# The layout of the second layer's normalised tokens: by position in the chunk, restored at the copies out of PSUM

## The chip, the cores and the metric

One core of one Trainium2 chip runs the whole program. The metric is the device time of one execution in microseconds. The core has TensorE (matrix products, PE in the profile; PEld is its weight loads), VectorE (DVE), ScalarE (ACT), GpSimd (POOL) and the queue SyncE (SP), which only issues DMAs here.

## What is computed

A two-layer streaming encoder step for one prompt of 2048 tokens and eight streams of 16 tokens, 2176 tokens of width 1024 in all, in float32. Layer 0 is a diagonal state-space mixer, layer 1 a gated delta rule. Cut to what the change touches, layer 1 is:

```
h    = rms_norm(x, norm_g[1]) * (1 + scale) + shift            # scale, shift from c
proj = h @ w_in                                                # 1024 -> 3088
qkv, z, b_raw, a_raw = split(proj)                             # 2048, 1024, 8, 8
full = concat([conv_hist, qkv], axis=1)
conv = sum(full[:, j:j + L] * conv_w[j] for j in range(4))     # along the tokens
act  = silu(conv)                                              # q, k, v of the heads
o, S = gated_delta_rule(q, k, v, sigmoid(b_raw), g(a_raw), S0)
out  = (rms_norm(o, norm_g) * silu(z)) @ w_out
```

The product `h @ w_in` runs over tokens in any order; the convolution needs them in order.

## The kernel before, in words

*Layout of the tokens.* 2176 tokens are 272 chunks of 8 (256 of the prompt, 16 of the streams). Layer 0 works by position in the chunk: its output for position j of all 272 chunks is one tile of 272 columns, and it runs through the positions backwards, j from 0 to 7 for position 7 - j. What layer 1 needs is normalised there and stored to DRAM as `h_d`, rows by channel, `[1024, position, 272]`. Position 0, the last, stays in SBUF.

*The tiles of layer 1.* For each of the 8 channel blocks k of 128 there is a high part `h1h` and a low part `h1l` (`h = h1h + h1l`, both of the type that the products take), in three tiles each by group g of chunks (`CG`, L840): 128, 96 and 48 chunks. `slots` (L836) gives the view of such a tile by position `s` and chunk `c`. `load_h(k)` (L854) loads one k from `h_d` into `xk`; `split_h` (L848) then writes, for each group, the high part by a cast on ScalarE (L851) and the low part by a subtraction on an engine E (L852), VectorE unless `load_h` is given another. k = 0 to 2 are loaded while layer 0 still runs, k = 3 to 7 at L1303 and L1312; k = 5 and 7 are split by GpSimd. k = 5 and 6 are loaded into tiles of layer 0's last products; k = 7 shares its tile `xk` with k = 3.

*Block 0 of the projection.* `first_block(k)` (L1294) multiplies the first 128 columns of `w_in` with positions 1 to 7 of channel block k, for five pieces of tokens (`NATT`: 512, 512, 384, 384, 384, of which 7/8 is 448 and 336), three products each: high by high, high weights by low, low weights by high. It accumulates over k in five PSUM tiles, in an order that is written out (`T.ordered`). Between k = 0 and 1 stand the products of the last position's norm. At the end position 0 is normalised on VectorE and ScalarE (L1314 to L1323, results `gh`, `gl`), multiplied (`pc_s`, L1324), and copied into the first position of the tiles `h1h` and `h1l`, by ScalarE (L1329) and GpSimd (L1330).

*Blocks 1 to 15, b/a and the gate.* `conv_block(b)` multiplies all tokens of a piece by 128 more columns (L1374), copies the result out of PSUM on ScalarE (L1378; L1380 for the tokens of the streams) into one row of tokens `pb`, and runs the convolution on VectorE (L1386, L1388), silu, squares (`sqf`) and stores on ScalarE. TensorE sums the squares (`pr`, L1407) inside the next block. In blocks 2 to 8 ScalarE also brings a copy of layer 0's output into token order (`x1_order`, L1427: load `x1k` on SP, copy `x1n` at L1433, store). The next weights come from `load_blk` (L842): a load `wdr` on SP, a cast on ScalarE (L135), a subtraction on VectorE (L137). `gate_cols` (L1587) does the same for the gate's eight blocks with silu straight out of PSUM, and the loop at L1460 for the 16 columns b/a.

*The order.* A scheduler places the instructions of each engine by its own estimate of when their inputs are ready, apart from stretches that the program orders by hand; each engine and each DMA queue then runs its list in that order.

The step of the moving operand in block 0 and the view that the splits write are these two lines:

```
1297    h, l = (t[k].rearrange("p (c s) -> p s c", s=8)[:, 1:8] for t in hcols(n0, n))
 838    return [t[g].rearrange("p (c s) -> p s c", s=8) for t in h]
```

Of the kernel before, what the change touches and what calls it, by code (L numbers as in the profile page):

```python
# [13 lines left out]
AF = mybir.ActivationFunctionType  # L14
# [39 lines left out]
def kernel(ctx: ExitStack, tc: tile.TileContext, I, O, upto="Z"):  # L54
# [19 lines left out]
    T, V, S, G, SY = (Engine(e) for e in (nc.tensor, nc.vector, nc.scalar, nc.gpsimd, nc.sync))  # L74
# [158 lines left out]
    with ExitStack() as pa:  # L233
# [337 lines left out]
        for j in range(8):  # L571
            hh, hl = hcur
            T.ordered = j == 1
            for cb in range(8):
# [14 lines left out]
                if j > 0:  # L589
                    ps = psd4.tile([P, NCH], F32, tag="d", name=f"pd{j}_{cb}")  # L590
# [221 lines left out]
    with ExitStack() as px:  # L812
# [20 lines left out]
                 for g in order for k in ks_ for i in "hl"}  # L833
            return [[[t[k, i, g] for g in range(3)] for i in "hl"] for k in ks_]

        def slots(h, g):  # L836

            return [t[g].rearrange("p (c s) -> p s c", s=8) for t in h]

        CG = (slice(0, 128), slice(128, 224), slice(224, NCH))  # L840

# [5 lines left out]

        def split_h(h, s0, sn, src, E):  # L848
            for g in range(3):
                hv, lv = (t[:, s0:s0 + sn] for t in slots(h, g))  # L850
                S.copy(hv, src[:, :, CG[g]])  # L851
                E.tensor_sub(lv, src[:, :, CG[g]], hv.bitcast(F32))  # L852

# [55 lines left out]
        for j in range(8):  # L909
# [3 lines left out]
            for ob in range(8):  # L913
                zt = (c4 if j else c3).tile([P, NCH], F32, tag="zt", name=f"zt{j}_{ob}")
                nc.sync.dma_start(zt, z_d[j][ob])
                ps = psc.tile([P, NCH], F32, tag="d", name=f"pg{j}_{ob}")
# [13 lines left out]
            else:  # L930
# [14 lines left out]
                hh_ = h_tiles((hpa, hpa, hpa), range(3), (0, 1, 2))  # L945
# [20 lines left out]
            for ob in range(8):  # L966
                if ob > 1:
                    project_out(ob)
                ps = pso_[ob]
# [304 lines left out]
    with pd:  # L1274
# [2 lines left out]
        hpb1 = rpool(ph1, "hpb1", 1)  # L1277
        hh_ += h_tiles((hpb1, hpb, hpb), range(3, KC), (0, 2, 1))

        def hcols(n0, n):  # L1280

            g = sum(8 * q.stop <= n0 for q in CG)
            c = n0 - 8 * CG[g].start
            return [[h[i][g][:, c:c + n] for h in hh_] for i in range(2)]

        psmp.__exit__(None, None, None)
        pd1 = pd.enter_context(ExitStack())
# [6 lines left out]
        def first_block(k):  # L1294
            for i in (0, 3, 4, 1, 2):
                n0, n = NATT[i]
                h, l = (t[k].rearrange("p (c s) -> p s c", s=8)[:, 1:8] for t in hcols(n0, n))
                ps = first[i][:, 0:7 * n // 8]
                T.matmul(ps, lhsT=wnext[0][:, k], rhs=h, start=(k == 0), stop=False)
                T.matmul(ps, lhsT=wnext[0][:, k], rhs=l, start=False, stop=False)  # L1300
                T.matmul(ps, lhsT=wnext[1][:, k], rhs=h, start=False, stop=(k == KC - 1))

        lds = [load_h(3), load_h(4), load_h(5, G), load_h(6)]  # L1303
        T.ordered = True
        first_block(0)
        norm(pss.tile([P, 512], F32, tag="s", name="msc")[:, 0:NCH])
# [2 lines left out]
        for k in range(3, KC):  # L1309
            lds[k - 3](hh_[k])  # L1310
            if k == 3:
                lds.append(load_h(7, G))  # L1312
            first_block(k)
        V.tensor_mul(xs, xs, bc(r[:, NPC:NCH].rearrange("p (q h) -> p q h", h=2), 1, 8))  # L1314
        V.tensor_mul(xs, xs, bc(gs1[:, :, 1:9], 3, 2))
# [9 lines left out]
        T.ordered = False  # L1325
        for g in range(3):
            for k in range(KC):
                hv, lv = (t[:, 0] for t in slots(hh_[k], g))
                S.copy(hv, h0[0][:, k, CG[g]].bitcast(F32))  # L1329
                G.tensor_copy(lv, h0[1][:, k, CG[g]].bitcast(F32))  # L1330
        xap.__exit__(None, None, None)
# [18 lines left out]
        def conv_block(b, w, hooks={}):  # L1350
            hi, lo = w
            pbt = pbp.tile([P, 2204], F32, tag="pb", name=f"pb_{b}")
            G.memset(pbt[:, 0:3], 0.0)
            pbs = pbt[:, 2051:2203].rearrange("p (q s) -> p q s", q=8)
            G.tensor_copy(pbs[:, :, 0:3], hist[:, b])
            sqf = i_ = None
            if b < 8:
                sqf = sqp.tile([P, NTOK], F32, tag="sqf", name=f"sqf{b}")
            for i0, (n0, n) in enumerate(NATT):
                npr = min(n, 2048 - n0)  # L1360
                if b == 0:

                    ps, c0 = first[i0][:, 0:7 * n // 8].rearrange("p (s c) -> p c s", s=7), n0 // 8
                    pv = pbt[:, 3 + n0:3 + n0 + npr].rearrange("p (c s) -> p c s", s=8)
                    S.copy(pv[:, :, 1:8], ps[:, 0:npr // 8])
                    S.copy(pv[:, :, 0], first0[:, c0:c0 + npr // 8])
                    if npr < n:
                        for h in range(2):
                            S.copy(pbs[:, :, 4 + 8 * h:11 + 8 * h],
                                   ps[:, npr // 8:].rearrange("p (q h) s -> p q h s", h=2)[:, :, h])  # L1370
                            S.copy(pbs[:, :, 3 + 8 * h], first0[:, NPC:NCH].rearrange("p (q h) -> p q h", h=2)[:, :, h])
                else:
                    ps = psd1.tile([P, 512], F32, tag="d", name=f"pc{b}_{n0}")[:, 0:n]
                    i_ = mm3(ps, [hi[:, k] for k in range(KC)], [lo[:, k] for k in range(KC)],  # L1374
                             *hcols(n0, n))
                    for f in hooks.get(i0, ()):
                        f(i_)
                    S.copy(pbt[:, 3 + n0:3 + n0 + npr], ps[:, 0:npr])  # L1378
                    if npr < n:
                        S.copy(pbs[:, :, 3:19], ps[:, npr:n].rearrange("p (q s) -> p q s", q=8))  # L1380
                ac = d3.tile([P, 512], F32, tag="ac", name=f"ac{b}_{n0}")[:, 0:n]
                parts = [(ac[:, 0:npr], lambda j: pbt[:, n0 + j:n0 + j + npr])]
                if npr < n:
                    parts.append((ac[:, npr:n].rearrange("p (q s) -> p q s", q=8), lambda j: pbs[:, :, j:j + 16]))
                for o, src in parts:
                    V.tensor_scalar(o, src(0), convw[:, b, 0:1], None, op0=ALU.mult)  # L1386
                    for j in range(1, 4):
                        V.scalar_tensor_tensor(o, src(j), convw[:, b, j:j + 1], o, op0=ALU.mult, op1=ALU.add)  # L1388
                S.activation(ac, ac, AF.Silu)
                if b < 8:  # L1390
                    store_heads(kq_d, (b + 4) % 8, n0, n, ac)
                    S.activation(sqf[:, n0:n0 + n], ac, AF.Square)
                else:
                    store_heads(v_d, b - 8, n0, n, ac)
            G.tensor_copy(hout[:, b, 0:3], pbt[:, 2048:2051])
            G.tensor_copy(hout[:, b, 3:27].rearrange("p (q s) -> p q s", q=8), pbs[:, :, 16:19])
            if b >= 8:
                return None
            rw = sqp.tile([P, 512], F32, tag="rw", name=f"rw{b}")


            def sums(after):
                pr = pss.tile([P, 512], F32, tag="s", name=f"pr{b}")
                pl = pss.tile([P, 4], F32, tag="s", name=f"prl{b}")
                with tc.issue_after(after):
                    for tt in range(4):
                        T.matmul(pr[32 * tt:32 * tt + 32, :], lhsT=one1, rhs=sqf[:, tt * 512:(tt + 1) * 512],  # L1407
                                 start=True, stop=True, tile_position=(0, 32 * tt))
                    T.matmul(pl, lhsT=sqf[:, 2048:2176], rhs=one1[:, 0:4], start=True, stop=True)
                V.tensor_copy(rw, pr)  # L1410
                V.tensor_copy(ssq[:, 16, b:b + 1], pl[:, 0:1])

            def turned(after):
                pt = pss.tile([P, 4, P], F32, tag="s", name=f"prt{b}")
                with tc.issue_after(after):
                    for o in range(4):
                        T.transpose(pt[:, o, :], rw[:, o * P:(o + 1) * P], ident)
                V.tensor_copy(ssq[:, 0:16, b].rearrange("p (t o) -> p o t", o=4),
                              pt.rearrange("p o (t r) -> p o t r", r=32)[:, :, :, 0])

            return sums, turned, i_

        with ExitStack() as pq:
# [37 lines left out]
            br = pbp.tile([P, 2204], F32, tag="pb", name="br")  # L1461
            for i0, (n0, n) in enumerate(NATT):
                ps = psd1.tile([P, 512], F32, tag="d", name=f"pba{n0}")[0:32, 0:n]
                hh, hl = hcols(n0, n)
                for k in range(KC):
                    T.matmul(ps, lhsT=wcat[:, k, :], rhs=hh[k], start=(k == 0), stop=False)
                    i_ = T.matmul(ps[0:16], lhsT=wcat[:, k, 0:16], rhs=hl[k], start=False, stop=(k == KC - 1)).ins
                S.copy(br[0:32, n0:n0 + n], ps)
                if i0 in (1, 3):
                    rows_of[7][i0 // 2](i_)  # L1470

# [115 lines left out]
        def gate_cols(b, w, n0, n, pool, tag):  # L1587
            ps = pool.tile([P, 512], F32, tag=tag, name=f"pz{b}_{n0}")[:, 0:n]
            mm3(ps, [w[0][:, k] for k in range(KC)], [w[1][:, k] for k in range(KC)], *hcols(n0, n))
            ac = d3.tile([P, 512], F32, tag="ac", name=f"az{b}_{n0}")[:, 0:n]  # L1590
            silu = S.activation(ac, ps, AF.Silu).ins
            store_heads(zz_d, b - 16, n0, n, ac)
            return silu

# [460 lines left out]
```

## Time and profile before

| what | value |
|---|---|
| device time, median of 3 runs | 2189.59 us (2188.38 to 2193.19) |
| the profiled execution's own time | 2189.92 us |
| span of the profiled execution, first to last instruction | 2188.2 us |
| mean granted clock of TensorE, share of full speed | 0.985 |
| busy: TensorE, its weight loads | 2122.6 us (97%), 1856.6 us (85%) |
| busy: VectorE, ScalarE, GpSimd | 1552.6, 962.2, 485.4 us |

The profile is of one execution. Times in its rows are microseconds from the start of the span. Layer 1 begins near 1015, block 1 of the projection at 1058, and the gate's last products end near 1690. A row's "x" is a count; "idle before" is the time that the engine stood idle ahead of the row, and the name behind the arrow is what ended it. [...]

### The profile page before, as it was taken

What the parts mean: (1) busy time and instruction counts of PE and PEld (TensorE: products, weight loads), DVE (VectorE), ACT (ScalarE), POOL (GpSimd) and SP (SyncE); (2) the same over time, 40 slices, a digit from 0 to 9 for tenths busy, and PEclk for the clock granted to TensorE, in tenths of its full rate; (3) what the DMA queues carried; (4) which work ended last, traced back from release to release, by engine and by line L of the source; (5) the groups of instructions that cost most, each with busy time, mean ns of one, the idle gap of its engine ahead of it and who ended that gap; (6) DMA issues with size and microseconds to landing.
All of it is one profiled execution on the core that took longest, in us unless ns stands there. A gap on an engine that the chain in (4) does not pass through costs nothing. (4 is left out here: it accounts for less than half of the span.)

```text
span 2188.2 us, 41752 instructions
## 1 busy us (share of the span) xinstructions
PE 2122.6 (97%) x15601; PEld 1856.6 (85%) x15601; DVE 1552.6 (71%) x3975; ACT 962.2 (44%) x2209; POOL 485.4 (22%) x731
## 2 busy tenths in 40 slices
PE   6999999999999999999999999999999799999998
PEld 4889987778789999998787879889987688888887
DVE  7999488777775444557654669687556888888885
ACT  3543422222254444447554432332223566666663
POOL 1156410000013222222300001100011244444430
PEclk8999999999999999999999999999999899999999
DMA  9796854444473333336455322563456644454532
GB/s 274 241 304 229 253 160 136 145 139 146 129 233 126 108 108 108 116 99 215 117 175 156 103 63 72 142 167 106 133 165 200 202 124 130 139 144 144 144 111 68
DMA packets 388295, 332.36 MB, mean 152 GB/s; under 512 B 87259, under 2 KB 349931, under 8 KB 388093
## 3 DMA queue, kind: packets, MB, share of 16 engines
q1 hardware_dynamic: 259084, 226.56, 35.2%
q10 hardware_dynamic: 126192, 95.49, 13.8%
q0 software_dynamic: 2816, 7.65, 1.0%
q8 instruction: 123, 2.02, 0.4%
q14 instruction: 80, 0.65, 0.1%
HBM read 213.01 MB, written 116.61 MB: 151 GB/s over the span
## 5 line engine op out<-in xcount | busy, mean ns | idle before, releaser
L149 PE MATMUL pc<-h1h,wdh 128*128 128x512 f32 (+1 forms) x600 | 217.1, 362 | 0.0
L151 PE MATMUL pc<-h1h,wdl 128*128 128x512 f32 (+1 forms) x600 | 216.7, 361 | 0.0
L150 PE MATMUL pc<-h1l,wdh 128*128 128x512 f32 (+1 forms) x600 | 215.9, 360 | 0.0
L1388 DVE SCALAR_TENSOR_TENSOR ac<-pb,convw,ac 128x384 f32<-128x384 f32 (+3 forms) x288 | 164.3, 593 | 3.6
L149 PE MATMUL pdz<-hhz,wzh 128*128 128x272 f32 x512 | 151.7, 298 | 0.0
L150 PE MATMUL pdz<-hlz,wzh 128*128 128x272 f32 x512 | 151.5, 297 | 0.0
L151 PE MATMUL pdz<-hhz,wzl 128*128 128x272 f32 x512 | 151.1, 296 | 0.0
L149 PE MATMUL po<-gh,woh 128*128 128x272 f32 x512 | 148.1, 290 | 1.3 <-ACT gh L926 1.3
L150 PE MATMUL pg<-yl,wgh 128*128 128x272 f32 x512 | 148.3, 290 | 0.0
L149 PE MATMUL pg<-yh,wgh 128*128 128x272 f32 x512 | 147.0, 288 | 1.3 <-ACT evz L630 1.3
L151 PE MATMUL po<-gh,wol 128*128 128x272 f32 x512 | 148.1, 289 | 0.0
L150 PE MATMUL po<-gl,woh 128*128 128x272 f32 x512 | 147.5, 288 | 0.0
L151 PE MATMUL pg<-yh,wgl 128*128 128x272 f32 x512 | 147.4, 288 | 0.0
L149 PEld LDWEIGHTS pc<-h1h,wdh 128*128 128x128 f32 x600 | 114.0, 190 | 10.2 <-PE pc L151 0.8
L150 PEld LDWEIGHTS pc<-h1l,wdh 128*128 128x128 f32 x600 | 113.8, 190 | 10.1 <-issue 0.8
L151 PEld LDWEIGHTS pc<-h1h,wdl 128*128 128x128 f32 x600 | 113.9, 190 | 9.7
L149 PE MATMUL pd<-hh,wuh 128*128 128x272 f32 x384 | 112.7, 294 | 0.1
L1386 DVE TENSOR_SCALAR ac<-pb,convw 128x512 f32<-128x512 f32 (+2 forms) x96 | 39.1, 421 | 103.4 <-ACT pb L1378 62.5
L69 PE MATMUL epo<-w2h,ohi 128*128 128x512 f32 x272 | 111.7, 410 | 0.0
L150 PE MATMUL pd<-hl,wuh 128*128 128x272 f32 x384 | 110.8, 289 | 0.3 <-DVE hl L230 0.3
L151 PE MATMUL pd<-hh,wul 128*128 128x272 f32 x384 | 110.9, 289 | 0.0
L69 PE MATMUL epo<-w2h,olo 128*128 128x512 f32 x272 | 106.9, 393 | 0.0
(610 smaller groups left out, 6378.5 us busy)
## 6 DMA issues: line engine op xcount, KB each, us to landing
wa<-in_w_ada SPq DMA_DIRECT2D x32, 512.0 KB
wdr<-in_w_in SPq DMA_DIRECT2D x24, 512.0 KB
h_d<-x ACTq DMA_DIRECT2D x8, 1088.0 KB
u_d<-ev ACTq DMA_DIRECT2D x64, 136.0 KB
hz<-h_d SPq DMA_DIRECT2D x16, 544.0 KB
u<-u_d SPq DMA_DIRECT2D x16, 544.0 KB
z_d<-evz ACTq DMA_DIRECT2D x64, 136.0 KB
y_d<-y ACTq DMA_DIRECT2D x32, 272.0 KB
```

Of the source, the lines that this page charges most:

```text
L69: i_ = f(*a, **kw)
L149: T.matmul(ps, lhsT=w_hi[k], rhs=x_hi[k], start=(k == 0), stop=False)
L150: T.matmul(ps, lhsT=w_hi[k], rhs=x_lo[k], start=False, stop=False)
L151: i_ = T.matmul(ps, lhsT=w_lo[k], rhs=x_hi[k], start=False, stop=(k == n - 1))
L1386: V.tensor_scalar(o, src(0), convw[:, b, 0:1], None, op0=ALU.mult)
L1388: V.scalar_tensor_tensor(o, src(j), convw[:, b, j:j + 1], o, op0=ALU.mult, op1=ALU.add)
```

## The change

The tiles `h1h` and `h1l` are kept as `p (s c)`: all chunks' tokens of position 0 first, then those of position 1, and so on, within each group. The splits and the copies of position 0 then write neighbouring words. `hcols` hands out a view of positions and chunks, 8 (or, in block 0, 7) runs of 64 or 48 neighbouring words, or one run where a piece is a whole group. A piece's result stands in PSUM in that order, and the copies out of PSUM, and the gate's silu, read it back by token. Besides, the splits of k = 5 and 7 go from GpSimd to VectorE.

```diff
-        def slots(h, g):
+        def slots(t, g):
-            return [t[g].rearrange("p (c s) -> p s c", s=8) for t in h]
+            return t[g].rearrange("p (s c) -> p s c", s=8)
...
         def split_h(h, s0, sn, src, E):
             for g in range(3):
-                hv, lv = (t[:, s0:s0 + sn] for t in slots(h, g))
+                hv, lv = (slots(t, g)[:, s0:s0 + sn] for t in h)
                 S.copy(hv, src[:, :, CG[g]])
                 E.tensor_sub(lv, src[:, :, CG[g]], hv.bitcast(F32))
...
-        def hcols(n0, n):
+        def hcols(n0, n, s0=0):
             g = sum(8 * q.stop <= n0 for q in CG)
-            c = n0 - 8 * CG[g].start
-            return [[h[i][g][:, c:c + n] for h in hh_] for i in range(2)]
+            c = slice(n0 // 8 - CG[g].start, (n0 + n) // 8 - CG[g].start)
+            return [[slots(h[i], g)[:, s0:, c] for h in hh_] for i in range(2)]
+        def by_token(ps, n):
+            return ps.rearrange("p (s c) -> p c s", c=n // 8)
...
-                h, l = (t[k].rearrange("p (c s) -> p s c", s=8)[:, 1:8] for t in hcols(n0, n))
+                h, l = (t[k] for t in hcols(n0, n, 1))
...
-        lds = [load_h(3), load_h(4), load_h(5, G), load_h(6)]
+        lds = [load_h(3), load_h(4), load_h(5), load_h(6)]
...
-                lds.append(load_h(7, G))
+                lds.append(load_h(7))
...
-                    S.copy(pbt[:, 3 + n0:3 + n0 + npr], ps[:, 0:npr])
+                    pv = by_token(ps, n)
+                    S.copy(pbt[:, 3 + n0:3 + n0 + npr].rearrange("p (c s) -> p c s", s=8), pv[:, 0:npr // 8])
                     if npr < n:
-                        S.copy(pbs[:, :, 3:19], ps[:, npr:n].rearrange("p (q s) -> p q s", q=8))
+                        S.copy(pbs[:, :, 3:19].rearrange("p q (h s) -> p q h s", h=2),
+                               pv[:, npr // 8:].rearrange("p (q h) s -> p q h s", h=2))
...
-                S.copy(br[0:32, n0:n0 + n], ps)
+                S.copy(br[0:32, n0:n0 + n].rearrange("p (c s) -> p c s", s=8), by_token(ps, n))
...
-            silu = S.activation(ac, ps, AF.Silu).ins
+            silu = S.activation(ac.rearrange("p (c s) -> p c s", s=8), by_token(ps, n), AF.Silu).ins
```

What this does to the order of the instructions is shown at three places. In the rows, `h1l_0` is the low part in group 0, the number behind it tells the tiles of one k apart, and `xk_12813`, `xk_12816` and `xk_12875` are the loads of k = 5, 6 and 7.

VectorE, from the reciprocal of the last position's norm to the end of the splits, in the kernel before:

```order
L990 RECIPROCAL acc_12475<-acc_12475 128x272
L137 TENSOR_TENSOR wdl_13111<-wdr_13112,wdh_13110 128x1024
L1314 TENSOR_TENSOR xa_12473<-xa_12473,acc_12475 128x8x16
L1321 SCALAR_TENSOR_TENSOR xa_12473<-acc_12475,gs_171,xa_12473 128x256
L1315 TENSOR_TENSOR xa_12473<-xa_12473,gs_171 128x8x16
L852 TENSOR_TENSOR h1l_0_12769<-xk_12816,h1h_0_12768 128x7x128
L1316 TENSOR_TENSOR xa_12473<-xa_12473,dsh 128x8x16
L852 TENSOR_TENSOR h1l_1_12789<-xk_12816,h1h_1_12788 128x7x96
L852 TENSOR_TENSOR h1l_2_12779<-xk_12816,h1h_2_12778 128x7x48
L1321 SCALAR_TENSOR_TENSOR xa_12473<-acc_12475,gs_171,xa_12473 128x256 x7
L1323 SCALAR_TENSOR_TENSOR gl_12993<-xa_12473,modT,gh_12992 128x272 x8
```

The same place with the change, from the first split behind the weights' (the line numbers are three higher from here on):

```order
L852 TENSOR_TENSOR h1l_0_12767<-xk_12813,h1h_0_12766 128x896
L1317 TENSOR_TENSOR xa_12473<-xa_12473,acc_12475 128x8x16
L1324 SCALAR_TENSOR_TENSOR xa_12473<-acc_12475,gs_171,xa_12473 128x256
L852 TENSOR_TENSOR h1l_1_12787<-xk_12813,h1h_1_12786 128x672
L852 TENSOR_TENSOR h1l_2_12777<-xk_12813,h1h_2_12776 128x336
L852 TENSOR_TENSOR h1l_0_12769<-xk_12816,h1h_0_12768 128x896
L852 TENSOR_TENSOR h1l_1_12789<-xk_12816,h1h_1_12788 128x672
L1318 TENSOR_TENSOR xa_12473<-xa_12473,gs_171 128x8x16
L852 TENSOR_TENSOR h1l_2_12779<-xk_12816,h1h_2_12778 128x336
L852 TENSOR_TENSOR h1l_0_12771<-xk_12875,h1h_0_12770 128x896
L852 TENSOR_TENSOR h1l_1_12791<-xk_12875,h1h_1_12790 128x672
L852 TENSOR_TENSOR h1l_2_12781<-xk_12875,h1h_2_12780 128x336
```

The splits of k = 5 and 7 now stand on VectorE, before seven of the eight operations at L1324 (L1321 before) and all eight at L1326 (L1323 before); a split is one run of elements instead of seven rows.

GpSimd, from the last sums of the norm on, as a difference:

```order
 L982 TENSOR_TENSOR acc_12475<-acc_12475,sqc 128x272 x6
-L852 TENSOR_TENSOR h1l_0_12767<-xk_12813,h1h_0_12766 128x7x128
-L852 TENSOR_TENSOR h1l_1_12787<-xk_12813,h1h_1_12786 128x7x96
-L852 TENSOR_TENSOR h1l_2_12777<-xk_12813,h1h_2_12776 128x7x48
-L852 TENSOR_TENSOR h1l_0_12771<-xk_12875,h1h_0_12770 128x7x128
-L852 TENSOR_TENSOR h1l_1_12791<-xk_12875,h1h_1_12790 128x7x96
-L852 TENSOR_TENSOR h1l_2_12781<-xk_12875,h1h_2_12780 128x7x48
```

Only the casts of position 0 are left there.

TensorE, at the end of the 24 products `pc_s` of position 0 and the start of block 1 (`pc_0` is block 1's first piece), in the kernel before:

```order
L69 MATMUL pc_s<-gh_12992,wdh_12417 128x272
L69 MATMUL pc_s<-gl_12993,wdh_12417 128x272
L69 MATMUL pc_s<-gh_12992,wdl_12418 128x272
L149 MATMUL pc_0_13191<-h1h_0_12399,wdh_13110 128x512
L150 MATMUL pc_0_13191<-h1l_0_12400,wdh_13110 128x512
L151 MATMUL pc_0_13191<-h1h_0_12399,wdl_13111 128x512
```

And with the change, from the thirteenth `pc_s` on:

```order
L69 MATMUL pc_s<-gh_12992,wdh_12417 128x272
L149 MATMUL pc_0_13191<-h1h_0_12399,wdh_13110 128x512
L150 MATMUL pc_0_13191<-h1l_0_12400,wdh_13110 128x512
L151 MATMUL pc_0_13191<-h1h_0_12399,wdl_13111 128x512
L149 MATMUL pc_0_13191<-h1h_0_12401,wdh_13110 128x512
L69 MATMUL pc_s<-gl_12993,wdh_12417 128x272
L69 MATMUL pc_s<-gh_12992,wdl_12418 128x272
L69 MATMUL pc_s<-gh_12992,wdh_12417 128x272
L150 MATMUL pc_0_13191<-h1l_0_12402,wdh_13110 128x512
L151 MATMUL pc_0_13191<-h1h_0_12401,wdl_13111 128x512
L149 MATMUL pc_0_13191<-h1h_0_12403,wdh_13110 128x512
```

Before, all 24 `pc_s` stand ahead of block 1; with the change, eleven of them stand behind its first products, and 14 products of block 1 stand ahead of the last `pc_s`. Past block 2 the order on TensorE is the same, and on SP's queue it is the same throughout.

## Rows read from the trace of the kernel before

**Rows 1.** The page's shares of the span: busy time, share and instructions by engine.
```profile
PE 2122.6 (97%) x15601; PEld 1856.6 (85%) x15601; DVE 1552.6 (71%) x3975; ACT 962.2 (44%) x2209; POOL 485.4 (22%) x731
```

**Rows 2.** Stretches: length, busy PE, PEld, DVE, ACT, POOL, then clock, DMA, GB/s.
```profile
1015.60:1036.00 20.40, 20.40 (x67) 13.19 (x66) 17.22 (x24) 17.47 (x22) 7.47 (x5) 1.00 0.66 231
...
1161.00:1223.40 62.40, 56.36 (x272) 47.94 (x271) 29.52 (x58) 30.66 (x41) 1.42 (x8) 0.95 0.57 169
```

**Rows 3.** Timeline of TensorE in block 0: start, duration, line, operation.
```profile
1022.08 0.57 PE L69 MATMUL pc<-h1h,wdl 128*128 128x448 f32 x1
1022.46 0.48 PE L69 MATMUL pc<-h1h,wdh 128*128 128x336 f32 x1
1022.74 0.48 PE L69 MATMUL pc<-h1l,wdh 128*128 128x336 f32 x1
```

**Rows 4.** The same timeline in block 1; one matmul left out between each two.
```profile
1058.14 0.39 PE L149 MATMUL pc<-h1h,wdh 128*128 128x512 f32 x1
...
1058.59 0.39 PE L151 MATMUL pc<-h1h,wdl 128*128 128x512 f32 x1
...
1070.08 0.33 PE L149 MATMUL pc<-h1h,wdh 128*128 128x384 f32 x1
...
1070.43 0.33 PE L151 MATMUL pc<-h1h,wdl 128*128 128x384 f32 x1
```

**Rows 5.** Groups by shape, ScalarE and VectorE, 993 to 1062: busy, mean ns.
```profile
L851 ACT CAST h1h<-xk 128x896 fp32r<-128x896 f32 x6 | 11.7, 1946 | 2.4 <-DMA xk<-h_d 2.4
...
L135 ACT CAST wdh<-wdr 128x1024 fp32r<-128x1024 f32 x3 | 3.1, 1044 | 2.5 <-PE pc_s L69 2.0 <-DMA wdr<-in_w_in 0.6
...
L852 DVE TENSOR_TENSOR h1l<-xk,h1h 128x896 fp32r<-128x896 f32 x4 | 7.8, 1959 | 2.9 <-ACT h1h L851 2.9
...
L137 DVE TENSOR_TENSOR wdl<-wdr,wdh 128x1024 fp32r<-128x1024 f32 x3 | 3.6, 1206 | 7.7 <-ACT wdh L135 7.7
```

**Rows 6.** Timeline of VectorE, 1028 to 1053, equal operations merged.
```profile
1028.96 1.85 DVE L990 RECIPROCAL acc<-acc 128x272 f32<-128x272 f32 x1
...
1031.80 2.66 DVE L1314 TENSOR_TENSOR xa<-xa,acc 128x128 f32<-128x128 f32 x1
...
1046.62 2.85 DVE L1321 SCALAR_TENSOR_TENSOR xa<-acc,gs,xa 128x256 f32<-128x256 f32 x7
1049.38 3.42 DVE L1323 SCALAR_TENSOR_TENSOR gl<-xa,modT,gh 128x272 fp32r<-128x272 f32 x8
```

**Rows 7.** Timeline of GpSimd in the same stretch.
```profile
1031.46 6.05 POOL L852 TENSOR_TENSOR h1l<-xk,h1h 128x896 fp32r<-128x896 f32 x3 [12.68 <-ACT h1h L851]
1038.77 7.29 POOL L852 TENSOR_TENSOR h1l<-xk,h1h 128x896 fp32r<-128x896 f32 x3 [1.25 <-ACT h1h L851]
1049.95 7.70 POOL L1330 CAST h1l<-gl 128x128 fp32r<-128x128 f32 x24 [3.90 <-DVE gl L1323]
```

**Rows 8.** Waits, 1058 to 1291: who for whom, us in total, times, longest.
```profile
ACT x1n L1433 <- DMA x1k<-x_d: 48.6, 16, 7.2
...
PE pr L1407 <- ACT sqf L1392: 5.8, 2, 4.2
```

**Rows 9.** Timeline of ScalarE behind the last product of position 0.
```profile
1058.21 1.05 ACT L135 CAST wdh<-wdr 128x1024 fp32r<-128x1024 f32 x1 [1.99 <-PE pc_s L69]
...
1067.11 2.35 ACT L1433 COPY x1n<-x1k 128x1088 f32<-128x1088 f32 x1 [7.19 <-DMA x1k<-x_d]
```

**Rows 10.** Timeline of SP's queue, 1031 to 1062.
```profile
1031.92 29.01 SPq L133 DMA_DIRECT2D wdr<-in_w_in  x2
```

**Rows 11.** Groups by shape, ScalarE's copies: busy, mean ns (1054 to 1056; 1058 to 1291).
```profile
L1365 ACT COPY pb<-pc 128x448 f32<-128x448 f32 x2 | 1.1, 560 | 0.0
...
L1378 ACT COPY pb<-pc 128x512 f32<-128x512 f32 x16 | 9.0, 579 | 2.2 <-ACT ac L1389 2.2
...
L1433 ACT COPY x1n<-x1k 128x1088 f32<-128x1088 f32 x16 | 36.9, 2309 | 48.6 <-DMA x1k<-x_d 48.6
```

**Rows 12.** Products over 256 columns, two runs and one: duration ns min/median/max.
```profile
L69 PE MATMUL epg<-ekl,ekh x48: 279/283/283, 1758.1 to 2073.8; 128*128 128x256 f32 x48
...
L69 PE MATMUL pks<-Sh,ekh x48: 278/279/388, 1772.6 to 2088.8; 128*128 128x256 f32 x48
```

More of the change, by code (lines that the diff above doesn't have):

```diff
@@ L1327 @@
             for k in range(KC):
-                hv, lv = (t[:, 0] for t in slots(hh_[k], g))
+                hv, lv = (slots(t, g)[:, 0] for t in hh_[k])
                 S.copy(hv, h0[0][:, k, CG[g]].bitcast(F32))
```

## Prediction

> **What bounds the kernel now.** I read the page's shares first: TensorE is busy for 97% of the span, VectorE for 71% [rows 1]. So a change pays where it shortens TensorE's own work, or where TensorE waits. The table of stretches says which holds around the change: in the first twenty microseconds of the second layer TensorE is busy for all 20.40 us at a granted clock of 1.00, and it is idle for 6.04 of 62.40 us between 1161 and 1223 [rows 2]. The first is the stage that the change rewrites, the second will take some of the gain back.
>
> In the first stage TensorE computes block 0 of the projection, chunk k by chunk k. From start to start, a matmul over 448 tokens takes 0.38 us and one over 336 takes 0.28 us [rows 3], so 0.84 ns a token. The same products in block 1 take 0.225 us for 512 tokens and 0.175 us for 384 (each two starts apart, halved) [rows 4], so 0.45 ns. The clock is the same and so are the types; what differs is the moving operand. In block 0 it is read as `p s c` out of a tile kept as `p (c s)`, that is, with a step of eight words between neighbours; in block 1 its tokens lie next to each other. The same step stands in the splits that write these tiles: ScalarE takes 1.946 us for 896 elements and 1.044 us for 1024 weights without a step, VectorE 1.959 against 1.206 us [rows 5]. GpSimd's splits cost VectorE more than themselves: while GpSimd works on three of them for 6.05 us [rows 7], VectorE needs 2.66 us for a product of 128 elements, against 2.85 us for seven operations of 256 elements when GpSimd is idle [rows 6].
>
> **The change, part by part.**
>
> *Block 0 on TensorE.* Each of 8 chunks k issues 3 products over 2 pieces of 448 and 3 of 336. Before: 24 x (2 x 0.38 + 3 x 0.28) = 38.4 us. After the change the operand is 7 runs of 64 or 48 neighbouring words. The price without a step comes from block 1: between 384 and 512 a token adds 0.39 ns, so 0.200 us for 448 and 0.156 us for 336. That gives 24 x (2 x 0.200 + 3 x 0.156) = 20.8 us, and TensorE has 17.6 us less to do in a stretch in which it never waits.
>
> *Whether the splits keep up.* A k takes 2.6 us then. TensorE, which begins at 1015.6, would want k = 3 near 1024 (three k and the norm's short products), then a new one every 2.6 us, up to k = 7 at 1034.5 and the products `pc_s` at 1037. ScalarE's five sets of 1904 elements cost 1.044/1024 x 1904 = 1.9 us each, about 10 us; it is not the limit. VectorE gets all five sets, 1.206/1024 x 1904 = 2.2 us each or 11.2 us, and beside them the reciprocal and the weights' split (1.85 and 1.2), eight operations at L1321 (8 x 2.85/7 = 3.3) and eight at L1323 (3.4) [rows 6], and three small ones at L1314 to L1316, which I put at 0.2 each since nothing of GpSimd's is left beside them. That is 21.5 us. It starts near 1018.5, after the last outputs of layer 0, and ends near 1040. TensorE's order needs its last result only near 1042 (the order shows that eleven of the 24 `pc_s` now stand behind products of block 1). k = 5, 6 and 7 come out of VectorE some 1.5 to 2 us ahead of their use. So I count no wait, but the margin is thin. The queue of loads on SP keeps its order; the load for k = 7 waits until k = 3 is split, and that is earlier than now. The 24 casts of the first token of a chunk stay on GpSimd; they end at 1057.65, 4.85 us behind VectorE's last operation [rows 6, 7], and TensorE needs them in their order, eight for block 1's first product, so their cover is `pc_s` and that product.
>
> *What starts later than TensorE does.* Here the gain shrinks. ScalarE's cast of the next weights waits for the last `pc_s` (1.99 us at 1058.21), and x1n, the first piece of the chain behind it, waits 7.19 us for its load [rows 9], whose place on SP's queue is behind the second weight load, held for most of 29.01 us [rows 10]. From there blocks 0 to 6 run through ScalarE, VectorE and SP at their own pace: ScalarE waits 48.6 us for x1k loads, in order, with the copies out of PSUM queued behind, and TensorE, faster, catches up and waits 5.8 us for `sqf` in the end [rows 8]. That chain begins with the last `pc_s`. TensorE is 17.6 us earlier there, but 14 products of 0.225 us now stand between the `pc_s`, so the last one ends 3.2 us later than it could: 1058.1 - 17.6 + 3.2 = 1043.7, which is 14.4 us earlier than now. TensorE then waits 3.2 us longer at `sqf`. The gain that reaches block 7 and all that follows is 14.4 us.
>
> *Copies out of PSUM.* In blocks 1 to 15, in the eight gate blocks and in the b/a block they now read with a step of n/8 words, eight at a time. The trace has that form already: block 0's copies read 448 tokens so, seven at a time, in 0.560 us, against 0.579 us for 512 without a step [rows 11]. Per token that is 1.25 against 1.13 ns, some 0.05 us a copy. The bounds are nothing and a doubling: the nearest strided copy in SBUF, x1n, takes 2.309 us for 1088, twice the rate of a plain one [rows 11]. I take 0.05 us, since that row has the same memory, step and engine. Of 35 such copies in blocks 1 to 7 (1.8 us) some lie in the chain: 0.5 us.
>
> [...]
>
> *The later products.* Their operand becomes eight runs of 64 or 48 words (one run in the last piece). The trace shows runs of 128: 283 ns with two runs, 279 with one [rows 12], so a break costs between nothing and 4 ns. I take nothing, since block 0's products have seven runs too and cost 0.84 ns a token at both lengths, with no fixed part left for the breaks.
>
> *Sum.* The profiled execution took 2189.9 us, 0.3 above the median of the runs shown. 2189.9 - 17.6 + 3.2 + 0.5 = 2176.0; against the median, **2175.7 us**.
>
> **The rivals.**
>
> *The chain does not hold TensorE back* (it has slack, or its loads fall better), and the whole 17.6 us arrives: 2172. For it: TensorE waits for `sqf` in two places only. Against: that it waits there already [rows 8].
>
> *The splits are late.* If VectorE's splits, now free of the step, stay at the durations that they have (1.96 us for 896, in proportion 4.1 for a set), its 21.5 us become 31 and end at 1049.5; the last `pc_s` follows near 1051, and 7 us are left: 2182.5. For it: all of GpSimd's share goes to VectorE. Against: the weights' split.
>
> *Copies out of PSUM at the doubled price.* 2176 tokens a block at 0.579/512 are 2.5 us; twice that adds 2.5 us a block to ScalarE, which the chain waits for, 17 us over blocks 1 to 7: 2192.5, no change that can be measured. It decides if the step costs over 0.3 us a copy. [...]
>
> *Broken runs slow the later products.* This is the way to a slower kernel. Blocks 1 to 15, eight gate blocks and b/a hold 4 x (360 + 192 + 16) = 2272 products with seven breaks each. At 4 ns a break that is 63 us on an engine that is busy throughout: 2238. It turns the sign at 0.9 ns a break (14 us over 15,900 breaks). For it: 283 against 279 ns. Against: block 0's products, though they run at half the pace.
>
> *The half pace has another cause than the step,* so that the change does not do what it says: 2189.
>
> **How the numbers follow.** Forecast 0.60, whole gain 0.13, late splits 0.13, dearer copies 0.05, broken runs 0.06, no effect 0.03. A measurement of this kernel can tell 0.2%, 4.4 us, from no change. Faster are the first three, 0.86; within it the dearer copies and no effect, 0.08; slower the broken runs, 0.06. The range takes the first three in, 2169 (the whole gain, and up to 3 us off TensorE's wait for `sqf`) to 2183 (late splits).
>
> **What the next profile should show.** Block 0's products 0.20 and 0.156 us apart; VectorE's splits of 896 near 1.1 us, none on GpSimd, and L1317 at a fraction of a microsecond; the cast behind `pc_s` near 1043.7; copies out of PSUM under 0.65 us for 512; block 1's products still 0.225 us apart; TensorE's wait for `sqf` between 1150 and 1210 grown to about 9 us. The forecast is wrong if TensorE waits for h1l inside block 0, if the products of 512 rise, or if the wait for `sqf` does not grow.

## Result and profile after

The changed kernel takes 2173.49 us (median of 4 runs, 2172.72 to 2174.6), the kernel before, measured beside it, 2188.99 us (4 runs, 2186.05 to 2193.19). The ratio is 0.9932, with a 95% interval from 0.9918 to 0.9945: faster by 15.5 us. Forecast were 2175.7 us, 2169 to 2183. A second measurement, with 6 runs of the changed kernel and 17 of the kernel before, gave 2172.3 against 2187.82, ratio 0.9927 (0.9916 to 0.9938).

The two profiled executions differ by 17.2 us (spans of 2188.2 and 2171.0). To see where, I marked each trace where TensorE starts its first product of a block, and took the distances (us):

| | block 0 to 2 | 2 to 5 | 5 to 8 | 8 and b/a | 9 to gates | to the last product |
|---|---|---|---|---|---|---|
| before | 68.32 | 77.38 | 87.38 | 42.48 | 179.35 | 709.19 |
| after | 52.32 | 77.36 | 86.82 | 42.45 | 181.62 | 707.33 |
| difference | -16.00 | -0.02 | -0.56 | -0.03 | +2.27 | -1.86 |

That makes 16.2 us from block 0 on; the other 1.0 us lies ahead of block 0, whose start lies anywhere between 1013.8 and 1018.5 us in the thirteen traces of this study, so it is not put down to the change. The gain is there at block 2 and stays. Block 9 to the gates, with its wait for `kt` loads (3.3 us before, 4.4 after), lies between 179.3 and 182.0 us in all of these traces, of either layout, so its 2.27 us are not put down to the change; nor is the last column (706.1 to 709.4).

The page of the changed kernel, its shares of the span; TensorE has 15.8 us less to do than in [rows 1]:

```profile
PE 2106.8 (97%) x15601; PEld 1853.3 (85%) x15601; DVE 1534.3 (71%) x3981; ACT 947.7 (44%) x2209; POOL 473.9 (22%) x725
```

The stretches that answer to [rows 2], same columns:

```profile
1014.60:1035.40 20.80, 20.80 (x122) 19.98 (x121) 18.70 (x37) 15.01 (x32) 0.10 (x1) 1.00 0.58 214
...
1143.60:1205.90 62.30, 56.65 (x274) 47.72 (x273) 29.48 (x58) 29.82 (x40) 1.43 (x8) 0.95 0.56 166
```

In 20.8 us, busy throughout, TensorE now gets through 122 matmuls, nearly all of them block 0's, where 20.4 us held 67 before. The second stretch, which begins with block 5, has lost nothing and gained next to nothing: 5.65 us idle in 62.3, against 6.04 in 62.4.

TensorE's timeline, in block 0 and in block 1 (start, duration, line, operation):

```profile
1018.50 0.36 PE L69 MATMUL pc<-h1h,wdl 128*128 128x448 f32 x1
1018.71 0.32 PE L69 MATMUL pc<-h1h,wdh 128*128 128x336 f32 x1
1018.86 0.32 PE L69 MATMUL pc<-h1l,wdh 128*128 128x336 f32 x1
...
1045.72 0.39 PE L149 MATMUL pc<-h1h,wdh 128*128 128x512 f32 x1
1045.95 0.39 PE L150 MATMUL pc<-h1l,wdh 128*128 128x512 f32 x1
```

From start to start (the durations, 0.32 to 0.39 us here, overlap), a product of 448 stands 0.21 us ahead of the next, one of 336 0.15 (0.38 and 0.28 in [rows 3]), and block 1's stand 0.23 apart as in [rows 4], though their operand is now eight runs of 64.

The splits, by shape, from 975 to 1050 (busy, mean ns, idle before):

```profile
L852 DVE TENSOR_TENSOR h1l<-xk,h1h 128x896 fp32r<-128x896 f32 x6 | 6.5, 1083 | 1.4 <-ACT h1h L851 1.4
...
L851 ACT CAST h1h<-xk 128x896 fp32r<-128x896 f32 x6 | 5.6, 940 | 2.3 <-DMA xk<-h_d 2.3
```

VectorE's and ScalarE's timelines at the end of the splits:

```profile
1026.04 0.28 DVE L1317 TENSOR_TENSOR xa<-xa,acc 128x128 f32<-128x128 f32 x1
...
1035.50 3.63 DVE L1326 SCALAR_TENSOR_TENSOR gl<-xa,modT,gh 128x272 fp32r<-128x272 f32 x8
```

```profile
1043.26 1.05 ACT L135 CAST wdh<-wdr 128x1024 fp32r<-128x1024 f32 x1 [1.00 <-PE pc_s L69]
...
1052.18 2.30 ACT L1438 COPY x1n<-x1k 128x1088 f32<-128x1088 f32 x1 [7.21 <-DMA x1k<-x_d]
```

Both splits run at about twice the pace of [rows 5] (1.083 us against 1.959 on VectorE, 0.940 against 1.946 on ScalarE), the product at L1317 takes 0.28 us against 2.66 in [rows 6], VectorE is through at 1039.1, and the cast behind `pc_s`, with x1n behind it, comes 14.9 us earlier than in [rows 9].

The waits from 1040 to 1273 that answer to [rows 8]:

```profile
ACT x1n L1438 <- DMA x1k<-x_d: 47.0, 15, 7.2
...
PE pr L1412 <- ACT sqf L1397: 4.4, 1, 4.4
PE pc L149 <- ACT pb L1382: 1.2, 1, 1.2
```

TensorE waits 5.6 us there, against 6.1 before (5.8 for `sqf`, 0.3 for `ssq`). The copies that answer to [rows 11], by shape, the blocks' first and then block 0's:

```profile
L1382 ACT COPY pb<-pc 128x512 f32<-128x512 f32 x16 | 8.9, 578 | 2.3 <-ACT ac L1394 1.4 <-PE pc L151 0.9
...
L1368 ACT COPY pb<-pc 128x448 f32<-128x448 f32 x2 | 1.1, 530 | 0.0
```

578 ns with a step of n/8 words in PSUM, 579 without: restoring the order of the tokens costs ScalarE nothing. The gates' activations of 512 out of PSUM took 598 ns before and 598 after.

### The profile page after: what moved, and what is told of

The parts are those of the page before. It is cut to its first block, busy times and chain, and to the rows that moved or that the text cites. A ratio compares the mean times of both kernels' runs of the same rounds, so it can differ in the third digit from the quotient of the medians.

```text
span 2171.0 us, 41750 instructions
## 1 busy us (share of the span) xinstructions
PE 2106.8 (97%) x15601; PEld 1853.3 (85%) x15601; DVE 1534.3 (71%) x3981; ACT 947.7 (44%) x2209; POOL 473.9 (22%) x725
## 5 line engine op out<-in xcount | busy, mean ns | idle before, releaser
L151 PE MATMUL pc<-h1h,wdl 128*128 128x384 f32 (+1 forms) x600 | 217.1, 362 | 0.0
L150 PE MATMUL pc<-h1l,wdh 128*128 128x384 f32 (+1 forms) x600 | 216.5, 361 | 0.4 <-POOL h1l L1333 0.4
```

The source lines that it names most:

```text
L150: T.matmul(ps, lhsT=w_hi[k], rhs=x_lo[k], start=False, stop=False)
L151: i_ = T.matmul(ps, lhsT=w_lo[k], rhs=x_hi[k], start=False, stop=(k == n - 1))
```

## Experiments

Each was run beside the kernel before on one chip; where times of two measurements are set side by side, ratios to the kernel before are given. For the stretches of each trace see the table at the end of this section.

### Block 0 read with a step again, in the new tiles

```diff
-                h, l = (t[k] for t in hcols(n0, n, 1))
+                g, o = ((0, 128), (0, 512), (1, 96), (1, 384), (1, 384))[i]
+                h, l = (t[g][:, o:o + n].rearrange("p (c s) -> p s c", s=8)[:, 0:7] for t in hh_[k])
```

> The changed kernel, but block 0's products read their operand with a step of eight words out of the new tiles; the words are others than the reference wants, so block 0 of the output is left wrong, the number of columns and the splits stay. Theory (the step of the moving operand is the whole price): products 0.38 and 0.28 us apart again, block 0 takes 38.4 us, splits of 896 stay near 1.08 us on VectorE: 2189 to 2191. Rival (the faster splits made the gain): products stay 0.20 and 0.154 us apart, 2173.5.

2189.35 us, 1.0012 (1.0003 to 1.0022) of the kernel before: all of the gain is gone. TensorE's timeline in block 0, and VectorE's splits by shape:

```profile
1024.60 0.57 PE L69 MATMUL pc<-h1h,wdh 128*128 128x448 f32 x1
1024.97 0.57 PE L69 MATMUL pc<-h1l,wdh 128*128 128x448 f32 x1
```

```profile
L852 DVE TENSOR_TENSOR h1l<-xk,h1h 128x896 fp32r<-128x896 f32 x5 | 5.4, 1086 | 1.3 <-ACT h1h L851 1.3
```

The splits kept their 1.09 us, the products went back to 0.37 us, and TensorE waits nowhere in block 0. So in block 0 the step of the operand sets the pace of TensorE, and fast splits by themselves bring nothing.

### Which steps cost

```diff
+                    h, l = (x.rearrange("p (c q t) -> p q c t", q=4, t=2)[:, :, 0:q] for x in t)
...
+                    h, l = (x.rearrange("p (c q t) -> p q c t", q=2, t=4)[:, :, 0:q] for x in t)
...
+                    st = 1 << k
+                    h, l = (x.rearrange("p (a c s) -> p a s c", a=8 // st, s=st)[:, :, :, 0:q] for x in t)
```

> The changed kernel; block 0's products read, for each k, other words of the same tiles, so that block 0 of the output is left wrong: for k = 0 to 4 single words with a step of 1, 2, 4, 8 and 16 words (runs of 56 or 42), for k = 5 pairs of neighbours with a step of eight words, for k = 6 groups of four with a step of eight, for k = 7 as in the changed kernel. One look, for the distance from start to start of a product over 448 columns. Theory (any operand whose neighbours are not adjacent is read at half the pace): 0.20 us at a step of 1, 0.38 at 2, 4, 8 and 16, pairs and fours between the two. Rival (the price grows with the step, for example with the words fetched): 0.20 at a step of 1 or 2, 0.38 at 8, more at 16.

This is one execution (2183.82 us), read for its distances alone. Two products of 448 columns each, TensorE's timeline: step of 2 words, step of 16, pairs, groups of four:

```profile
1017.76 0.60 PE L69 MATMUL pc<-h1l,wdh 128*128 128x448 f32 x1
1018.16 0.60 PE L69 MATMUL pc<-h1h,wdl 128*128 128x448 f32 x1
...
1032.45 0.58 PE L69 MATMUL pc<-h1h,wdh 128*128 128x448 f32 x1
1032.83 0.57 PE L69 MATMUL pc<-h1l,wdh 128*128 128x448 f32 x1
...
1037.32 0.59 PE L69 MATMUL pc<-h1h,wdh 128*128 128x448 f32 x1
1037.72 0.59 PE L69 MATMUL pc<-h1l,wdh 128*128 128x448 f32 x1
...
1042.70 0.37 PE L69 MATMUL pc<-h1l,wdh 128*128 128x448 f32 x1
1042.91 0.37 PE L69 MATMUL pc<-h1h,wdl 128*128 128x448 f32 x1
```

0.40 us at a step of 2 (and of 4), 0.38 at 16 (and 8), 0.40 for pairs, 0.21 for groups of four words; runs of 56 took 0.20. The rival is out: the price doesn't grow with the step. The theory was right for single words and wrong for pairs and fours, which it put between the two: pairs cost the full price, fours none. Four neighbouring words are enough when four others lie between the groups; other distances between groups of four were not run.

### Late splits, with the fast operand

```diff
-                hv, lv = (slots(t, g)[:, s0:s0 + sn] for t in h)
+                c = CG[g].stop - CG[g].start
+                hv, lv = (t[g][:, c:].rearrange("p (c s) -> p s c", s=7)[:, s0 - 1:s0 - 1 + sn] for t in h)
```

> The changed kernel, but the splits write their results with a step of seven words over seven eighths of each tile; block 0 and the later blocks then read words in the wrong order, so the output is left wrong, while TensorE reads runs of neighbours as in the changed kernel. Theory (the prediction's rival of late splits, as a mechanism of its own: fast products need fast splits): splits of 896 take about 1.9 us again, VectorE's work before pc_s grows from 21.5 to some 31 us, TensorE waits 7 to 9 us in block 0: 2181 to 2184. Rival (the splits' pace does not matter, TensorE's step is all): 2173 to 2175.

2182.8 us, 0.9977 (0.9965 to 0.9988). VectorE's splits by shape, and TensorE's waits from 1014 to 1062:

```profile
L853 DVE TENSOR_TENSOR h1l<-xk,h1h 128x896 fp32r<-128x896 f32 x6 | 11.9, 1988 | 3.2 <-ACT h1h L852 3.2
```

```profile
PE pc L69 <- DVE h1l L853: 3.2, 3, 1.7
PE msc L69 <- ACT sqc L981: 1.8, 1, 1.8
PE pc_s L69 <- DVE gl L1327: 1.7, 1, 1.7
PE pc L150 <- POOL h1l L1334: 0.5, 1, 0.5
```

Block 0 to 2 takes 63.39 us, 11.07 more than after the change, where TensorE waited 0.4 us. Set beside each other product by product, 6.8 us of this are the longer waits, 1.6 us are products at the lower granted clock, 0.50 for 3.4 us from 1037.7 on, and 2.7 us lie in the products next to the waits, which stand farther apart. At the lower clock, TensorE's timeline:

```profile
1037.83 0.57 PE L69 MATMUL pc<-h1h,wdh 128*128 128x448 f32 x1
1038.20 0.57 PE L69 MATMUL pc<-h1l,wdh 128*128 128x448 f32 x1
```

Of 16 us only 5 are left. A fast operand without fast splits is worth a third of the change. The edit slows ScalarE's casts too (1.95 us for 896 again), and 1.8 us of the waits are for ScalarE's `sqc`; what VectorE's part alone would cost was not run.

### Only the other engine, only the other layout

The kernel before with the splits of k = 5 and 7 on VectorE, and the changed kernel with them on GpSimd:

```diff
-        lds = [load_h(3), load_h(4), load_h(5, G), load_h(6)]
+        lds = [load_h(3), load_h(4), load_h(5), load_h(6)]
...
-                lds.append(load_h(7, G))
+                lds.append(load_h(7))
```

> The kernel before, with the splits of k = 5 and 7 on VectorE too, and the old layout. Theory (TensorE bounds block 0 at its half pace, and VectorE's 31 us of splits end near 1049, before TensorE needs them): no wait of TensorE for h1l in block 0, 2187 to 2191. Rival (late splits): VectorE's splits of 1.96 us for 896 come late for k = 7 or for pc_s, TensorE waits 3 us or more: 2192 to 2196. Second rival (GpSimd's splits held VectorE up, so that taking them off GpSimd is a gain by itself): 2183 to 2186.

2190.05 us, 1.0014 (1.0004 to 1.0024): no gain. TensorE doesn't wait in block 0. Taking the work off GpSimd frees VectorE (0.30 us for a product of 128 elements, against 2.66 in [rows 6]), but VectorE is not what TensorE waits for. The product of 128 elements, on VectorE's timeline:

```profile
1034.91 0.30 DVE L1314 TENSOR_TENSOR xa<-xa,acc 128x128 f32<-128x128 f32 x1
```

Block 0 to 2 even takes 1.2 us more, which the section on the prediction comes back to.

> The changed kernel, with the splits of k = 5 and 7 given back to GpSimd, the new layout kept. Theory (the layout alone carries the gain in TensorE's pace, and VectorE alone was needed only so that the splits keep up with it): block 0 still wants a k every 2.6 us, GpSimd needs some 6 us for the three splits of one k (6.05 us before, with the step), so TensorE waits 2 to 4 us for h1l of k = 5 and again for k = 7, and VectorE's product of 128 elements beside GpSimd's splits takes over 2 us again instead of 0.28: 2176 to 2180. Rival (the engine does not matter): no wait in block 0, 2173.5.

2180.63 us, 0.9976 (0.9966 to 0.9986): the layout without the engine keeps about a third of the gain. The timelines of GpSimd and VectorE, and TensorE's waits from 1014 to 1062:

```profile
1026.71 10.67 POOL L852 TENSOR_TENSOR h1l<-xk,h1h 128x896 fp32r<-128x896 f32 x6 [10.31 <-ACT h1h L851]
```

```profile
1027.17 2.22 DVE L1317 TENSOR_TENSOR xa<-xa,acc 128x128 f32<-128x128 f32 x1
...
1032.02 3.00 DVE L852 TENSOR_TENSOR h1l<-xk,h1h 128x896 fp32r<-128x896 f32 x1
```

```profile
PE pc L69 <- DVE h1l L852: 3.5, 2, 2.3
PE pc L69 <- POOL h1l L852: 0.3, 1, 0.3
```

The expected waits came, but not where I expected them. GpSimd itself is late by only 0.3 us; it makes VectorE late: while GpSimd works, a split on VectorE takes 3.00 us instead of 1.08, the product of 128 elements 2.22 instead of 0.28, and k = 6, VectorE's own, costs TensorE 3.5 us. From block 0 to 8 the trace is 7.2 us longer than the changed kernel's; the ratio puts the loss nearer 10 us, and where the rest lies is not placed.

### pc_s ahead of block 1

```diff
-        mm3(first0, ks(wnext[0]), ks(wnext[1]), ks(h0[0]), ks(h0[1]))
+        pcs_last = mm3(first0, ks(wnext[0]), ks(wnext[1]), ks(h0[0]), ks(h0[1]))
...
+                    with later([pcs_last] if (b, i0) == (1, 0) else []):
+                        i_ = mm3(ps, [hi[:, k] for k in range(KC)], [lo[:, k] for k in range(KC)],
+                                 *hcols(n0, n))
```

> The changed kernel, with all 24 products pc_s of position 0 ahead of block 1's first product. Theory of the prediction (one chain begins with the last pc_s and runs at its own pace to block 7): the last pc_s ends near 1039.5 instead of 1042.3, the chain is 2.8 us earlier throughout, and the waits behind sqf (4.4 us) and behind the copy out of PSUM (1.2 us) shrink by 2.8 us together: about 2170.7. Rival (the chain is tied to TensorE anew in each block, at the cast of the next weights, so that its first start does not count): those waits stay between 5 and 6 us, and TensorE only loses about 1 us inside pc_s, since VectorE delivers gl every 0.46 us: 2173.5 to 2174.5.

2169.75 us, 0.9921 (0.9906 to 0.9936): not to be told from the changed kernel's 0.9927 to 0.9932. ScalarE's timeline, and TensorE's wait for `sqf`:

```profile
1042.49 0.24 ACT L1374 COPY pb<-pc_s 128x8 f32<-128x8 f32 x1
1042.55 1.12 ACT L135 CAST wdh<-wdr 128x1024 fp32r<-128x1024 f32 x1
```

```profile
PE pr L1413 <- ACT sqf L1398: 5.5, 2, 3.6
```

The last `pc_s` started at 1039.25 instead of 1043.06, but the cast only moved from 1043.26 to 1042.55, and without a wait: ScalarE is busy with its own casts and copies up to there. Of the 3.8 us the chain got 0.7, so this run doesn't decide between the theories by itself; it shows that the 14 products in front of the last `pc_s` cost the chain 0.7 us and not 3.2. The waits for `sqf` stayed at 5.5 us, as the rival had it, and TensorE lost nothing in `pc_s` but gained 0.6 us up to block 2.

### Two pieces of x1 a block instead of three

```diff
-                for i in range(3 * (b - 2), min(3 * (b - 1), 16)) if b > 1 else ():
+                for i in range(*[0, 0, 0, 2, 4, 6, 8, 10, 16][b:b + 2]):
```

> The changed kernel, with two pieces of x1 (load x1k, copy x1n) instead of three per block in blocks 2 to 6 and the six left over put into blocks 7 and 8. If it is the three pieces in ScalarE's queue that make a block of the chain longer (about 29 us) than TensorE's 25.3 us, a block of it falls to about 22 us, the waits behind sqf and the copy out of PSUM between 1143 and 1206 go, and with them the low clock behind them: blocks 5 to 7 take 62.3 us now against 2.5 blocks of 25.3 without a wait, so at most 11 us, 2162 to 2167. Rival (TensorE waits there for something else, or the wait moves to the loads kt at 1411 to 1417): 2172 to 2175.

2175.07 us, 0.9949 (0.9935 to 0.9963). Blocks 5 to 7, then block 8 and b/a (length, busy PE, PEld, DVE, ACT, POOL, clock, DMA share, GB/s), and TensorE's waits:

```profile
1148.38:1226.86 78.48, 77.87 (x404) 66.85 (x404) 40.55 (x80) 39.20 (x57) 2.08 (x12) 1.00 0.53 153
1226.86:1277.83 50.97, 44.96 (x233) 32.44 (x232) 27.25 (x57) 21.42 (x40) 4.36 (x15) 0.93 0.37 109
```

```profile
PE prt L1422 <- DVE rw L1415: 6.0, 2, 4.2
PE pr L1412 <- ACT sqf L1397: 0.6, 1, 0.6
```

Both sides were right about something: blocks 5 to 7 fell from 86.8 to 78.5 us as the theory of the three pieces says, and the six pieces left over made a new wait of 6.0 us in blocks 8 and b/a, 8.5 us longer than without. The one cancels the other: as a whole nothing is gained, and the time is the rival's.

So the pieces were given out two a block from block 1 on, with `pc_s` ahead of block 1, in two ways (the lists were `[0, 0, 2, 4, 6, 8, 10, 12, 16]` and `[0, 0, 2, 4, 6, 8, 10, 13, 16]`):

> The changed kernel with pc_s ahead of block 1 and the sixteen pieces of x1 given out two a block from block 1 on (four in block 7, none behind it). Theory (three pieces a block make ScalarE's queue longer than TensorE's 25.3 us a block; six left over at the end made TensorE wait 6 us for ssq in blocks 8 and b/a): blocks 5 to 7 take 76 to 79 us instead of 85, block 8 and b/a 42.5, about 2162 to 2164. Rival (the wait only moves: to sqf of block 6 or 7, or to ssq in block 8): 2168 to 2172.

2165.33 us, 0.9906 (0.9889 to 0.9924).

> The same with the pieces given out two a block up to block 5 and three in blocks 6 and 7. By the theory of the three pieces the load is evened a little differently: blocks 5 to 7 at 76 to 80 us, 2162 to 2165. By the rival, as with the pieces two a block, 2168 to 2172.

2169.17 us, 0.9922 (0.9907 to 0.9938), with 3.3 us of the wait for `sqf` back and no gain to be told from the changed kernel. The first was measured again, beside the changed kernel:

> pc_s ahead of block 1 and the pieces of x1 two a block, once more. By the theory of the three pieces blocks 5 to 7 take about 79 us instead of 87, so the kernel stands 6 to 9 us below the changed one measured beside it. If the earlier 0.9906 of the kernel before was chance, it stands within 2 us of it.

> The changed kernel once more, beside the next one on the same chip, for a comparison of the two: 0.993 of the time of the kernel before, and 5 to 6 us of waits behind sqf and copies out of PSUM in blocks 5 to 7.

2167.84 us against 2172.3: 0.9900 (0.9887 to 0.9913) and 0.9927 (0.9916 to 0.9938) of the kernel before. Blocks 5 to 7 of the one and of the other:

```profile
1148.58:1227.21 78.63, 78.03 (x403) 66.82 (x403) 41.85 (x83) 38.09 (x57) 2.08 (x12) 1.00 0.51 150
```

```profile
1146.13:1231.48 85.35, 80.67 (x404) 69.08 (x404) 45.07 (x88) 39.46 (x59) 2.07 (x12) 0.96 0.46 134
```

The intervals stand apart, if barely, so this version beats both kernels. The 6.7 us in blocks 5 to 7 are 4.1 us of waits (0.6 against 4.7 idle) and 2.6 us of busy time: the granted clock is 0.50 for 6.8 us from 1197.3 on, and 1.00 throughout in the other. Blocks 2 to 4 take 1.2 us more, and 1.0 us up to block 2 goes with `pc_s` and not with the pieces. The gain of 4.5 us is smaller than the 6 to 9 expected.

The stretches of all traces (us, as in the first table):

| | block 0 to 2 | 2 to 5 | 5 to 8 | 8 and b/a |
|---|---|---|---|---|
| changed, again | 52.58 | 77.36 | 85.35 | 42.45 |
| block 0 with a step of eight | 69.56 | 77.36 | 84.09 | 42.45 |
| other steps | 63.88 | 77.36 | 85.21 | 42.45 |
| late splits | 63.39 | 77.36 | 85.77 | 42.45 |
| old layout, VectorE alone | 69.53 | 77.46 | 86.29 | 42.48 |
| new layout, GpSimd | 56.82 | 79.29 | 87.61 | 42.45 |
| pc_s first | 51.72 | 77.34 | 84.95 | 42.45 |
| x1 two a block, rest behind | 52.25 | 78.54 | 78.48 | 50.98 |
| pc_s first, x1 two a block | 51.80, 51.60 | 78.52, 78.52 | 79.36, 78.63 | 42.45, 42.45 |
| the same, three in blocks 6, 7 | 51.83 | 78.52 | 81.74 | 42.45 |

## Why the prediction was right, and where it was not

**Block 0 on TensorE: right.** The term was 38.4 to 20.8 us; from start to start the 120 products take 38.76 us before and 20.95 after, 17.8 us less. That the step causes it is shown by putting it back: 0.37 us for 448 columns again, and 69.56 us for block 0 to 2.

**The splits keep up: right, with the margin about as thin as said.** VectorE ended at 1039.1 (forecast 1040), TensorE never waits for it, and the low parts of k = 5 to 7 are ready 1.7 to 2.6 us ahead of their use (forecast 1.5 to 2). Late splits were put at 2182.5 us, with 7 us of the gain left; with late splits the kernel took 2182.8, with 5 us left. That the two times agree is partly luck, since the late splits cost more than forecast and the rest of the sum was too high. Only at the end was a cover a little short: the forecast had GpSimd's casts of position 0 hidden behind `pc_s` and block 1's first product, and TensorE waits 0.4 us for one of them. Block 1's products take 24.73 us instead of 23.82, and 0.7 of the 0.9 us lie in the two products around this wait; with `pc_s` ahead of them, they take 23.93.

**The chain: its start right, its effect wrong.** The cast was to come at 1043.7 and came at 1043.26. The step that failed is "TensorE then waits 3.2 us longer at `sqf`": the wait fell from 5.8 to 4.4 us, where about 9 were forecast, and by the prediction's own sign ("if the wait for `sqf` does not grow") this part is wrong. TensorE's start of block 2 came 2.1 us closer to that cast (23.65 us behind it, 25.71 before), yet blocks 5 to 7 did not grow. Across the traces with three pieces of x1 a block they take 84.1 to 87.6 us, and the two longest, 87.38 and 87.61, are those where TensorE leaves the chain most room, 25.7 and 25.6 us, the opposite of the forecast. Those with the same room, 23.6 to 23.7 us, still differ by 2.7 us, so single traces show no more than that the room is not what decides. What does change the wait is how many pieces of x1, with their loads, ScalarE's queue holds in each block: with two in place of three 6.7 to 8.3 us of that stretch go, wait and low clock together (0.6 us idle against 4.7 and 5.6, mean clock 1.00 against 0.96). Whether the copies or the loads count was not separated, and how the chain takes up 2 us of delay was not traced instruction by instruction; both stay open.

**What gave the gain back instead.** Of the 17.8 us, 16.0 arrive at block 2. Besides the 0.9 us in block 1 it is the products `pr`, which write 32 rows of the result each and are issued in small groups between block products. TensorE's timeline, before:

```profile
1077.46 1.05 PE L1407 MATMUL pr<-sqf,one 128*32 128x512 f32 x4
1078.44 0.45 PE L149 MATMUL pc<-h1h,wdh 128*128 128x384 f32 x1
```

And after:

```profile
1060.09 1.04 PE L1412 MATMUL pr<-sqf,one 128*32 128x512 f32 x2
1061.06 0.45 PE L150 MATMUL pc<-h1l,wdh 128*128 128x384 f32 x1
```

In both traces, ahead of block 5, a group takes 0.97 or 0.98 us with two, 0.98 with four and 0.99 to 1.00 with eight. Up to block 3 there were four groups (3.93 us) and are now five (4.90). Five stand in the old layout with the splits on VectorE too, four in the new one with the splits on GpSimd: it comes with the order that VectorE's splits lead to, not with the layout, and it explains most of the 1.2 us that the old layout lost with VectorE alone.

**Copies out of PSUM: 0.5 us too much.** The forecast took 0.05 us a copy from block 0's 448 columns; the price is nothing (578 against 579 ns). Block 0's copies, in which nothing changed, took 530 ns after and 560 before, so the row that the forecast took moves by more than half of its price by itself. ScalarE reads with a step of n/8 words at the pace that it has without one, 1.13 ns a token, and nothing of the rival's doubled price shows.

**Broken runs: right.** Products of 512 stand 0.23 us apart with eight runs as with one, and blocks 2 to 4 take 77.36 against 77.38 us.

Together: the forecast gave back 3.7 us for chain and copies, the traces show 1.9 us in block 1 and `pr`, and 0.6 us gained at `sqf`. The rival "whole gain", 2172, lies 1.5 us from the median, the forecast 2.2, so the time alone does not tell them apart. The traces speak against the mechanism of either: something is given back, but not at `sqf`. That the forecast came so close is partly luck: 3.7 us were booked for causes that cost nothing here, and stood in for 1.9 us of causes that the sum did not have.

## What to carry to other kernels

Keep a tile in the order in which TensorE reads it, four neighbouring words at a time or more as far as these runs go (0.21 us for 448 columns, against 0.38 to 0.40 with pairs or single words), and put a reordering into ScalarE's copies out of PSUM, where it cost nothing (578 ns for 512 tokens, against 579). When TensorE gets faster, make sure that what feeds it gets faster too: operand and splits were worth 16 us together, but the fast operand alone 5 us and the fast splits alone nothing. Before a wait downstream is booked as a loss, find out what sets its length; here it went with the work in ScalarE's queue per block, and a plan for that queue, together with `pc_s` ahead of block 1, gained another 4.5 us.

## What was not expected of the hardware

Pairs of neighbouring words cost TensorE the full price, 0.40 us for 448 columns, as single words at a step of two or four do, and groups of four none, 0.21. Why four neighbours are enough and two are not, no run shows.

VectorE was slower beside GpSimd without any step as well: one split on VectorE took 3.00 us beside GpSimd's, and 1.08 alone.

TensorE's waits came with more than their length here. In blocks 5 to 7, 4.1 us more of waits in the changed kernel than with two pieces came with 2.6 us of slower work, the granted clock being 0.50 for 6.8 us. With late splits, 6.8 us more of waits came with 4.3 us more, 1.6 of them at the clock of 0.50.
